# Part of the adaLN modulation of a two-layer backbone: products on GpSimd and VectorE beside the first feed-forward network

## The chip, the cores and the metric

One core of a Trainium2 chip. The metric is the device time of one launch, in microseconds (us). The engines are TensorE (PE in the profile, PEld its weight loads), VectorE (DVE), ScalarE (ACT), GpSimd (POOL) and SyncE (SP). SP issues the large loads, GpSimd issues DMAs of its own.

## The reference, cut to what matters

Two layers over 256 latent and 256 context tokens of width 1024. Every sub-layer is normalised, scaled and shifted by six vectors that come from a conditioning vector, and gated when it is added back:

```python
mod   = silu(c)     @ mod_w + mod_b      # 6 x 1024 for the latent tokens
mod_c = silu(c_ctx) @ mod_w + mod_b      # 6 x 1024 for the context tokens
sh_m, sc_m, g_m, sh_f, sc_f, g_f = split(mod, 6)
h = rmsnorm(x, mix_pre) * (1 + sc_m) + sh_m
x = x + g_m * rmsnorm(mixer(h), mix_post)
h = rmsnorm(x, ffn_pre) * (1 + sc_f) + sh_f
x = x + g_f * rmsnorm(channel_mixer(h), ffn_post)
```

Layer 0 has a pooling and attention mixer and a dense SwiGLU network of hidden width 2816, layer 1 a gated DeltaNet and a top-2-of-8 expert network. The context tokens need no more than the first two vectors of layer 1.

## The kernel before

**Arithmetic.** Every weight slab of [128, 2048] is loaded by SP into a raw buffer and split into a high and a low part, [128, 1024] at a time: ScalarE rounds the high part (L235), VectorE subtracts it (L236, two inputs from SBUF). `wp` has three buffers for each part. A product is three matmuls, L246 to L248 in the up part, L241 to L243 in the down part.

**The first feed-forward network** (`ffn(1, ...)`, the context tokens) takes the 22 blocks of the hidden width two at a time, in eleven steps `s` = 0 to 10. A step is 96 matmuls of 256 columns (up, two slabs), from `s` = 1 on also 24 matmuls of 512 columns (down, one slab, the blocks of step `s`-1), and then `fill(s)`, other work that is put between the steps. A step has six weight halves, so six L235 and six L236. `fill(0)` normalises the latent tokens (its reciprocal root is a `pow` on GpSimd, L261), `fill(1)` transposes them (L293).

**The modulation.** `mod_w` is cut in twelve blocks `j` of 512 columns for each layer; vector `j // 2`, half `j % 2`. `mod_chunk` loads a block as two raw slabs, multiplies it on TensorE with the two conditioning vectors (L415: eight products with 32 columns of weights, each of them two instructions in the trace), copies the sum to SBUF (ScalarE, L433; for the gates, vectors 2 and 5, VectorE adds a bias, L421), and then transposes it into columns (L436, four transposes) or spreads it over the partitions (L430, one product for each conditioning vector) and multiplies by the norm's gain (L431). Before the change a block stands in each `fill(s)` of `s` = 0 to 8; block 10 of layer 0 stands ahead of step 0, and blocks 10, 11, 4 and 5 of layer 1 come in layer 1, from `gates()`.

**The order** of each engine's instructions is made when the program is built: a scheduler with a cost model of its own takes the recorded instructions, and allots the pools' buffers. On the chip every engine keeps that order, and an instruction that waits holds up all that stand behind it on its engine.

Of the kernel before, what the change touches and what calls it, by code (L numbers as in the profile page):

```python
# [10 lines left out]
F32 = mybir.dt.float32  # L11
# [26 lines left out]
NF = 1  # L38
# [71 lines left out]
def _layout(i):  # L110
    """Only data layout: slabs of 128 partitions x 2048 columns, in the order of use."""
# [54 lines left out]
def trunk(ctx, tc, I, out, dbg=None, stop=None):  # L166
# [27 lines left out]
    # ---- constants  # L194
# [31 lines left out]
    # ---- weights: slabs of [128, 2048] from DRAM, then exact high and low parts  # L226
# [12 lines left out]
    def mm3w(ps, ah, al, bh, bl, start, stop):  # L239
        """like mm3, with the low part of b as late as can be"""  # L240
        TE.matmul(ps, ah, bh, start=start, stop=False)  # L241
        TE.matmul(ps, al, bh, start=False, stop=False)  # L242
        TE.matmul(ps, ah, bl, start=False, stop=stop)  # L243
# [6 lines left out]
    # ---- adaLN modulation  # L250
# [3 lines left out]
    # ---- norms  # L254
# [26 lines left out]
    def to_hT(xns, r, ab, ps_of, name):  # L281
        """a stream's normalised tokens, transposed and modulated, as high and low parts; in parts"""
# [21 lines left out]
    def post_begin(ps, grow, ss, w2, junk_of=None):  # L304
        """the sum of squares of a half of y, in PSUM, and that half times its gain"""
        junk = (junk_of or w2)()
        S.activation(junk, ps, AF.Square, accum_out=ss)
        tmp = w2()
        V.tensor_mul(tmp, ps, grow)  # L309
        return tmp  # L310

    def post_end(x_, tmps, ss):
        """x += y * rstd(y)"""
# [7 lines left out]
    def post_residual(x_, halves, grow, w2):  # L321
        """x += (y * rstd(y)) * grow, y in two PSUM tiles."""
# [25 lines left out]
    def hT_tiles(n=T):  # L348
        """high and low parts of a [1024, n] activation, 128 rows to a plane"""
# [10 lines left out]
    def flow(*lanes, lead=False):  # L360
        """traces generators side by side, each at its rate, until all, or the first of them, have ended"""
# [19 lines left out]
    # =================================================== layer 0  # L381
# [27 lines left out]
    def mod_chunk(l, j, load=load, raws=None):  # L409
# [22 lines left out]
        else:  # L432
# [8 lines left out]
            if vec in (1, 4):  # L441
                if half == 0:
# [5 lines left out]
                                       op0=OP.add, op1=OP.mult)  # L448

# [9 lines left out]
    with ExitStack() as mx:  # L459
# [84 lines left out]
        def project():  # L544
            """keys and values, queries, then the channels of the pools"""
# [45 lines left out]
        def softmax(qt, kv):  # L591
            """the probabilities of four heads, rows of queries, in steps"""
# [43 lines left out]
        def read(qt):  # L636
            """the values that eight heads read, rows (group, channel) of the planes of w_out's rows"""
# [62 lines left out]
        early = []  # L700
        for n in range(2):
            for t in order:
                ys[t, n] = psA() if n == 0 else psB()
            for s in range(2):
                raw = slab0(I["w_out"][n, s])
                w = [split_w(raw[:, q * 1024:(q + 1) * 1024]) for q in range(2)]
                if n == 1 and s == 1:
                    early.append(mod_load("l0", 10, slab0))
# [28 lines left out]
    # =============================================== layer 0, FFN  # L737
    by_pow.append(True)

    def ffn(half, acc_of, up_of, load, fill=lambda s: None):  # L740
        """the FFN of one stream, two blocks of the hidden width at a time, in parts"""
# [60 lines left out]
    def fill(s):  # L802
        """other work between the parts of the first stream's FFN"""
# [6 lines left out]
        if mods:  # L810
            mod_chunk(*mods.pop(0), slab0)

    mods = [("l0", 11)] + [("l1", j) for j in (0, 1, 2, 3, 6, 7, 8, 9)]
# [3 lines left out]
    mod_chunk("l0", 10, raws=early.pop())  # L817

    def stream_hT(half, ps_of):
        """the FFN's residual; normalised, modulated and transposed tokens of one stream for layer 1, in parts"""  # L820
# [16 lines left out]
    def both(*gens):  # L837
        """two or more generators in step"""
# [13 lines left out]
    # =================================================== layer 1, gated DeltaNet  # L852
# [46 lines left out]
    def decays(half):  # L899
        """decay and write strength of every token of a stream: columns (direction, tile, head)"""  # L900
# [55 lines left out]
    def blocks(p_, c, half, ps_of):  # L956
        """projection of two heads: [channel, (head, token)]"""
# [10 lines left out]
    def conv_rows(p_, c, half, ps_of):  # L968
        """centred 5-tap convolution along the tokens, 2 * silu, rows of tokens (head, tile)"""
# [21 lines left out]
    def unit_rows(ps, dst, scale):  # L991
        """rows of 128 scaled to the length sqrt(scale); ps holds twice the values"""
# [15 lines left out]
    def staggered(gens, lag):  # L1008
        """traces several generators a step at a time, each lag steps behind the one before"""
# [18 lines left out]
    def project(us, half, ps_of):  # L1028
        """keys of all the pairs of heads first, then the rest; columns (head, tile)"""
# [56 lines left out]
    def scores(u):  # L1086
        """P[j, (direction, head), i] = beta_j (k_j . k_i) decay, strictly before i"""
# [45 lines left out]
    def eliminate(us):  # L1133
        """inverses of the 16 x 16 diagonal blocks of I + P, by elimination on all systems at once"""
# [15 lines left out]
        # forward systems are kept reversed, rows and columns, so that all of them run the same way  # L1150
# [18 lines left out]
    def inverse(u, t):  # L1169
# [26 lines left out]
        # join the two 64 x 64 halves  # L1196
# [28 lines left out]
    def scan(u):  # L1225
        """both directions through the two tiles of a stream, from the state that the last one left"""
# [68 lines left out]
    def gated(u):  # L1295
        """rms norm of every head, gain and gate; transposed parts for the output product"""
# [71 lines left out]
    def gates():  # L1368
        for m in (10, 11, 4, 5):
# [31 lines left out]
    def turned_logits(ps, src, first, last):  # L1401
        """adds the products of 512 channels of a tile of tokens and the router's columns"""
# [10 lines left out]
    def old_logits():  # L1413
        """the router's logits of the tokens before the mixer's part: the gain of the norm goes into the router's
        columns, the shift into a row that is added"""
# [57 lines left out]
    # =================================================== layer 1, experts  # L1473
# [3 lines left out]
    # slabs go round the two pools; a few of the first ones go where nothing else is needed yet  # L1477
# [21 lines left out]
    # the mixer's residual and the norm before the experts; the tokens' logits from those of the two summands  # L1499
# [354 lines left out]
```

## Time and profile before

| | us |
|---|---|
| runs (3) | 2088.44, 2089.57, 2093.78 |
| median | 2089.57 |
| span of the profiled execution | 2088.6 |
| TensorE busy | 1998.0 (96%) |
| VectorE busy | 1590.5 (76%) |
| ScalarE busy | 1354.4 (65%) |
| GpSimd busy | 115.0 (6%) |
| step 0 of the first feed-forward network begins, step 9 ends (TensorE) | 233.3, 440.8 |

How to read it: a matmul's busy time includes its pipeline, so neighbours overlap, and the distance between the starts of two matmuls is what one of them costs TensorE. Idle time matters on the engine that ends a stage. The whole span's averages mix stages of different limits; what counts here is the stretch from 225 to 441 us, in which GpSimd is nearly idle, and the later stretch around 725 to 825 us, in which two of the moved blocks stood.

### The profile page before, as it was taken

What the parts mean: (1) busy time and instruction counts of PE and PEld (TensorE: products, weight loads), DVE (VectorE), ACT (ScalarE), POOL (GpSimd) and SP (SyncE); (2) the same over time, 40 slices, a digit from 0 to 9 for tenths busy, and PEclk for the clock granted to TensorE, in tenths of its full rate; (3) what the DMA queues carried; (4) which work ended last, traced back from release to release, by engine and by line L of the source; (5) the groups of instructions that cost most, each with busy time, mean ns of one, the idle gap of its engine ahead of it and who ended that gap; (6) DMA issues with size and microseconds to landing.
All of it is one profiled execution on the core that took longest, in us unless ns stands there. A gap on an engine that the chain in (4) does not pass through costs nothing. (4 is left out here: it accounts for less than half of the span.)

```text
span 2088.6 us, 30619 instructions
## 1 busy us (share of the span) xinstructions
PE 1998.0 (96%) x11433; PEld 1659.6 (79%) x11433; DVE 1590.5 (76%) x2407; ACT 1354.4 (65%) x2069; POOL 115.0 (6%) x163
## 2 busy tenths in 40 slices
PE   6999899999999899999979999999999999999997
PEld 3746687889999788988868888788887888878785
DVE  3475544456667877886669999899989989899997
ACT  5254543446556566655458878788787777877775
POOL 0000000000001214212000000000000000000000
PEclk9999999999999999999979999999999999999998
DMA  8352467745554344113258999899999999999993
GB/s 352 121 199 80 169 221 260 258 168 170 177 182 162 122 136 168 61 62 104 79 192 309 370 352 361 330 366 374 343 350 350 369 357 354 355 353 369 347 378 124
DMA packets 74076, 519.78 MB, mean 249 GB/s; under 512 B 9456, under 2 KB 9616, under 8 KB 11584
## 3 DMA queue, kind: packets, MB, share of 16 engines
q1 hardware_dynamic: 72864, 515.51, 66.7%
q0 software_dynamic: 1056, 2.24, 0.4%
q8 instruction: 91, 1.49, 0.3%
q14 instruction: 65, 0.53, 0.1%
HBM read 516.67 MB, written 1.05 MB: 248 GB/s over the span
## 5 line engine op out<-in xcount | busy, mean ns | idle before, releaser
L236 DVE TENSOR_TENSOR wlo<-raw,whi 128x1024 fp32r<-128x1024 f32 x878 | 1056.0, 1228 | 266.3 <-ACT whi L235 233.9
L235 ACT ACTIVATE whi<-raw 128x1024 fp32r<-128x1024 f32 x878 | 926.0, 1060 | 467.2 <-PE psA L242 138.7
L243 PE MATMUL psA<-wlo,xh 128*128 128x512 f32 x896 | 354.2, 395 | 2.1 <-DVE wlo L236 2.1
L241 PE MATMUL psA<-whi,xh 128*128 128x512 f32 x896 | 353.3, 395 | 0.3 <-ACT whi L235 0.2
L242 PE MATMUL psA<-whi,xl 128*128 128x512 f32 x896 | 349.9, 391 | 0.0
L241 PE MATMUL psB<-whi,gh 128*128 128x512 f32 x536 | 212.4, 397 | 0.3 <-DVE yacc L1762 0.3
L242 PE MATMUL psB<-whi,gl 128*128 128x512 f32 x536 | 212.1, 396 | 0.0
L243 PE MATMUL psB<-wlo,gh 128*128 128x512 f32 x536 | 210.3, 396 | 0.0
L243 PEld LDWEIGHTS psA<-wlo,xh 128*128 128x128 f32 x896 | 168.2, 188 | 42.3 <-DVE wlo L236 7.5
L241 PEld LDWEIGHTS psA<-whi,xh 128*128 128x128 f32 x896 | 168.2, 188 | 34.8 <-ACT whi L235 1.5
L242 PEld LDWEIGHTS psA<-whi,xl 128*128 128x128 f32 x896 | 168.4, 188 | 33.9 <-DVE xl L1678 0.2
L241 PEld LDWEIGHTS psB<-whi,gh 128*128 128x128 f32 x536 | 100.8, 188 | 23.9 <-issue 0.7
L242 PEld LDWEIGHTS psB<-whi,gl 128*128 128x128 f32 x536 | 100.8, 188 | 23.2
L243 PEld LDWEIGHTS psB<-wlo,gh 128*128 128x128 f32 x536 | 100.3, 188 | 23.8
L246 PE MATMUL psB<-fh,whi 128*128 128x256 f32 x352 | 102.3, 291 | 0.0
L246 PE MATMUL psA<-fh,whi 128*128 128x256 f32 x352 | 100.6, 286 | 0.0
L247 PE MATMUL psB<-fl,whi 128*128 128x256 f32 x352 | 100.3, 285 | 0.0
L248 PE MATMUL psB<-fh,wlo 128*128 128x256 f32 x352 | 100.2, 285 | 0.0
L247 PE MATMUL psA<-fl,whi 128*128 128x256 f32 x352 | 99.6, 283 | 0.0
L248 PE MATMUL psA<-fh,wlo 128*128 128x256 f32 x352 | 99.6, 283 | 0.0
L261 POOL TENSOR_TENSOR rstd<-rstd,mhalf 128x1 f32<-128x1 f32 x17 | 13.1, 774 | 1379.5 <-DVE ss L1509 1005.3
L246 PE MATMUL psB<-jh,whi 128*128 128x256 f32 x256 | 75.6, 295 | 0.0
(474 smaller groups left out, 3447.1 us busy)
## 6 DMA issues: line engine op xcount, KB each, us to landing
raw<-in_moe SPq DMA_DIRECT2D x336, 1024.0 KB, 7.5
raw<-in_ffn SPq DMA_DIRECT2D x66, 1024.0 KB, 4.8
raw<-in_l_mod SPq DMA_DIRECT2D x48, 1024.0 KB, 5.0
raw<-in_w_qkvz SPq DMA_DIRECT2D x24, 1024.0 KB, 4.9
raw<-in_w_out SPq DMA_DIRECT2D x8, 1024.0 KB, 4.8
raw<-in_w_in SPq DMA_DIRECT2D x5, 1024.0 KB, 10.4
w<-in_l_post POOLq DMA_DIRECT2D x8, 256.0 KB, 3.5
x<-in_x SPq DMA_DIRECT2D x2, 512.0 KB, 5.0
```

The lines of the kernel that those rows point to most:

```text
L235: S.activation(hi, src, AF.Copy)
L236: V.tensor_sub(lo, src, f(hi))
L241: TE.matmul(ps, ah, bh, start=start, stop=False)
L242: TE.matmul(ps, al, bh, start=False, stop=False)
L243: TE.matmul(ps, ah, bl, start=False, stop=stop)
L246: TE.matmul(ps, ah, bh, start=start, stop=False)
L247: TE.matmul(ps, ah, bl, start=False, stop=False)
L248: TE.matmul(ps, al, bh, start=False, stop=stop)
L261: G.tensor_tensor(r, r, mhalf[:, 0:n], op=OP.pow)
```

## The change

Twelve blocks, here called c0 to c11, no longer go through `mod_chunk`: c0 and c1 are blocks 10 and 11 of layer 0, c2 to c5 are blocks 0 to 3 of layer 1, c6 to c9 its blocks 6 to 9, c10 and c11 its blocks 10 and 11. The first six have two conditioning vectors, the others one. `mod_begin` loads a block in eight tiles of [128, 512] by DMAs that GpSimd issues, into a pool of six buffers; for the first four tiles GpSimd multiplies by the conditioning vector's column (`tensor_scalar`) and adds to a [128, 512] accumulator (`tensor_tensor`). `mod_end` does the other four tiles on VectorE (`scalar_tensor_tensor`, both tensors in SBUF), then TensorE only sums over the partitions: for the gates by a product with a matrix of ones, otherwise by four transposes for each vector, which VectorE reduces. `fill(s)` begins 1, 1, 1, 1, 1, 2, 2, 2, 0, 0, 0 blocks and ends the oldest ones until two are left open, from `s` = 9 on all. So c0 ends in `fill(1)`, c1 in `fill(2)`, c2 and c3 in `fill(3)` and `fill(4)`, then c4 and c5, c6 and c7, c8 and c9 in pairs, and c10 and c11 in `fill(9)`.

```diff
+NM = 6
+MODS = (1, 1, 1, 1, 1, 2, 2, 2, 0, 0, 0)
+MLAG = 2
...
+    def mod_begin(l, j):
+        vec = j // 2
+        nr = 2 if l == "l0" or vec < 2 else 1
+        if vec in (2, 5):
+            nc.gpsimd.dma_start(bias0[0:1, :], I[l + "_modb"][j:j + 1, :])
+        accs_ = [w2() for r in range(nr)]
+        ws = []
+        for k in range(KD):
+            t = modp.tile([P, 512], F32, tag="modw", name="modw")
+            nc.gpsimd.dma_start(t, I[l + "_mod"][j, k // 4, :, (k % 4) * 512:(k % 4 + 1) * 512])
+            ws.append(t)
+        for k in range(4):
+            for r in range(nr):
+                c_ = cs[:, k, r:r + 1]
+                if k == 0 and vec not in (2, 5):
+                    G.tensor_scalar(accs_[r], ws[k], c_, None, op0=OP.mult)
+                else:
+                    part = modp.tile([P, 512], F32, tag="part", name="part", bufs=1)
+                    G.tensor_scalar(part, ws[k], c_, None, op0=OP.mult)
+                    G.tensor_tensor(accs_[r], accs_[r] if k else bias0, part, op=OP.add)
+        return l, j, accs_, ws[4:]
+
+    def mod_end(begun):
+        l, j, accs_, ws = begun
+        vec, half = j // 2, j % 2
+        for k in range(4, KD):
+            for r, a_ in enumerate(accs_):
+                V.scalar_tensor_tensor(a_, ws[k - 4], cs[:, k, r:r + 1], a_, op0=OP.mult, op1=OP.add)
+        if vec in (2, 5):
...
+                TE.matmul(ps, every, accs_[r], start=True, stop=True)
+                V.tensor_mul(dst, ps, post)
+            return
+        for r, a_ in enumerate(accs_):
+            ps = psB()
+            for b in range(4):
+                TE.transpose(ps[:, b * P:(b + 1) * P], a_[:, b * P:(b + 1) * P], ident)
+            V.tensor_reduce(colm[l][:, vec, half * 4:(half + 1) * 4, r:r + 1],
+                            ps.rearrange("p (b q) -> p b q", b=4), axis=AX.X, op=OP.add)
+        mod_finish_columns(l, vec, half, len(accs_))
...
-                if n == 1 and s == 1:
-                    early.append(mod_load("l0", 10, slab0))
...
-        if mods:
-            mod_chunk(*mods.pop(0), slab0)
-
-    mods = [("l0", 11)] + [("l1", j) for j in (0, 1, 2, 3, 6, 7, 8, 9)]
+        for _ in range(MODS[s]):
+            begun.append(mod_begin(*mods.pop(0)))
+        while len(begun) > (MLAG if s < 9 else 0):
+            mod_end(begun.pop(0))
+
+    mods = [("l0", 10), ("l0", 11)] + [("l1", j) for j in (0, 1, 2, 3, 6, 7, 8, 9, 10, 11)]
+    modp = l0.enter_context(tc.tile_pool(name="modp", bufs=NM))
...
+    begun = [mod_begin(*mods.pop(0))]
...
-    mod_chunk("l0", 10, raws=early.pop())
...
-        for m in (10, 11, 4, 5):
+        for m in (4, 5):
```

The order is the scheduler's, so the diff does not show it. Three places follow, with the program's buffer numbers; the changed kernel has other line numbers. First TensorE at the end of a step `s` = 4, of the kernel before, where a block of layer 1 stands behind the last down matmuls, and its transposes stand right behind its products:

```order
L243 MATMUL psA_2199<-wlo_2816,gh_2606 128x512
L415 MATMUL psB_2835<-raw_2831,cs_101 32x512 x4
L415 MATMUL psB_2835<-raw_2833,cs_101 32x512 x4
L436 MATMUL psB_2846<-cst_74,w2_2844 128x128 x4
L246 MATMUL psB_2857<-fh_1815,whi_2858 128x256
```

and the same place of the changed kernel, where c3's accumulators `w2_2532` and `w2_2533` are transposed:

```order
L243 MATMUL psA_2238<-whi_2957,gh_2713 128x512
L244 MATMUL psA_2238<-whi_2957,gl_2714 128x512
L245 MATMUL psA_2238<-wlo_2958,gh_2713 128x512
L508 MATMUL psB_3019<-cst_74,w2_2532 128x128 x4
L508 MATMUL psB_3025<-cst_74,w2_2533 128x128 x4
L248 MATMUL psB_3035<-fh_1859,whi_3036 128x256
```

The eight products are gone, and TensorE now waits at this place for the accumulators. Second, VectorE of the changed kernel in step 5, around c5 (accumulators `w2_2973` and `w2_2974`; `wlo` are the low parts of the network's weights, `raw_3095` is the second up slab of step 5 and `raw_3161` its down slab):

```order
L238 TENSOR_TENSOR wlo_3099<-raw_3095,whi_3098 128x1024
L456 TENSOR_TENSOR colm_l1_92<-colm_l1_92,modc_l1_90 128x8
L492 SCALAR_TENSOR_TENSOR w2_2973<-modw_2983,cs_101,w2_2973 128x512
L238 TENSOR_TENSOR wlo_3127<-raw_3095,whi_3126 128x1024
L492 SCALAR_TENSOR_TENSOR w2_2974<-modw_2983,cs_101,w2_2974 128x512
L492 SCALAR_TENSOR_TENSOR w2_2973<-modw_2985,cs_101,w2_2973 128x512
L492 SCALAR_TENSOR_TENSOR w2_2974<-modw_2985,cs_101,w2_2974 128x512
L238 TENSOR_TENSOR wlo_3164<-raw_3161,whi_3163 128x1024
```

A block's sums now stand between the low parts, so a low part that TensorE needs in this step stands behind a sum that needs GpSimd's part. Third, GpSimd of the changed kernel, from the last two instructions of c2 (`w2_2314`) into c3 (tiles `modw_2534` on), with what each waits for:

```order
L484 TENSOR_TENSOR w2_2314<-w2_2314,part_2348 128x512 [waits Pool_49]
L474 DMA modw_2536<-in_l1_mod 128x512
L474 DMA modw_2538<-in_l1_mod 128x512 [waits DMASW5_49,DVE_49]
L480 TENSOR_SCALAR w2_2532<-modw_2534,cs_101 128x512 [waits DMASW2_49,Activation_49]
L480 TENSOR_SCALAR w2_2533<-modw_2534,cs_101 128x512 [waits Activation_49]
L474 DMA modw_2540<-in_l1_mod 128x512 [waits DMASW6_49,DVE_49]
L474 DMA modw_2542<-in_l1_mod 128x512 [waits Pool_49]
L483 TENSOR_SCALAR part_2552<-modw_2536,cs_101 128x512 [waits DMASW3_49]
L496 DMA w2_2578<-in_l0_post 128x512 [waits DMASW7_49,Activation_49]
L484 TENSOR_TENSOR w2_2532<-w2_2532,part_2552 128x512 [waits Pool_49]
```

Before, GpSimd had nothing in this stretch but two small DMAs and a few `pow`. Now its loads of c3 stand between its products, and the third and fourth of them wait for VectorE to be done with the buffers of c2.

## Rows read from the trace of the kernel before

**Rows 1.** The page's busy times over the span, of TensorE and GpSimd.

```profile
PE 1998.0 (96%) x11433; PEld 1659.6 (79%) x11433; DVE 1590.5 (76%) x2407; ACT 1354.4 (65%) x2069; POOL 115.0 (6%) x163
```

**Rows 2.** Busy time by stretch: length, PE, PEld, DVE, ACT, POOL, clock, DMA share.

```profile
325.00:350.00 25.00, 24.28 (x181) 21.41 (x180) 11.10 (x14) 10.41 (x13) 0.00 (x0) 1.00 0.74 264
```

**Rows 3.** Timeline of TensorE in the first feed-forward network: start, length, instruction.

```profile
227.42 3.64 PE L415 MATMUL psB<-raw,cs 128*32 128x512 f32 x16 [0.20 <-ACT w L296]
231.00 0.86 PE L293 MATMUL psB<-cst,w 128*128 128x128 f32 x4
...
301.20 0.66 PE L436 MATMUL psB<-cst,w 128*128 128x128 f32 x4 [0.72 <-ACT w L433]
...
313.20 0.40 PE L241 MATMUL psA<-whi,gh 128*128 128x512 f32 x1
...
318.90 1.92 PE L415 MATMUL psB<-raw,cs 128*32 128x512 f32 x16
321.54 0.66 PE L436 MATMUL psB<-cst,w 128*128 128x128 f32 x4 [0.72 <-ACT w L433]
...
339.23 1.92 PE L415 MATMUL psB<-raw,cs 128*32 128x512 f32 x16
...
440.81 0.28 PE L246 MATMUL psB<-fh,whi 128*128 128x256 f32 x1
```

**Rows 4.** What TensorE waited for from 218 to 450 us: total, times, longest.

```profile
PE psB L436 <- ACT w L433: 7.2, 8, 2.2
PE psB L430 <- DVE rstd L260: 4.0, 1, 4.0
```

**Rows 5.** Instructions of GpSimd over the span: nanoseconds min/median/max; a landing; a pow.

```profile
L1178 POOL TENSOR_TENSOR w<-w,cst x8: 1273/1292/1507, 799.5 to 909.3; 128x512 f32<-128x512 f32 x8
...
L1175 POOL TENSOR_TENSOR u<-w,cst x32: 716/736/1729, 697.4 to 993.0; 128x256 f32<-128x256 f32 x32
...
L1106 POOL TENSOR_SCALAR_AFFINE_SELECT x<-x x12: 401/408/412, 599.8 to 882.9; 128x256 f32<-128x256 f32 x12
...
L424 POOL DMA_DIRECT2D w<-in_l_post x8: 547/600/673, 108.5 to 811.5; - x8
...
DMA to landing us min/median/max: 3.3/3.5/7.1
...
251.95 0.58 POOL L261 TENSOR_TENSOR rstd<-rstd,mhalf 128x1 f32<-128x1 f32 x1
```

**Rows 6.** VectorE: the low parts from 225 to 430 us, and a two-input sum of 512.

```profile
L236 DVE TENSOR_TENSOR wlo<-raw,whi x53: 1224/1226/1227, 237.7 to 427.8; 128x1024 fp32r<-128x1024 f32 x53
...
L985 DVE SCALAR_TENSOR_TENSOR u<-u,u x20: 680/685/1215, 543.0 to 956.6; 128x512 f32<-128x512 f32 x20
```

**Rows 7.** Timelines of GpSimd and VectorE where both work, in layer 1.

```profile
961.91 1.30 POOL L1178 TENSOR_TENSOR w<-g,cst 128x512 f32<-128x512 f32 x1
963.16 3.53 POOL L1178 TENSOR_TENSOR w<-x,cst 128x512 f32<-128x512 f32 x2
...
963.45 2.10 DVE L236 TENSOR_TENSOR wlo<-raw,whi 128x1024 fp32r<-128x1024 f32 x1 [4.11 <-ACT whi L235]
...
987.01 7.13 POOL L1175 TENSOR_TENSOR u<-w,cst 128x256 f32<-128x256 f32 x8
...
990.66 1.76 DVE L236 TENSOR_TENSOR wlo<-raw,whi 128x1024 fp32r<-128x1024 f32 x1 [1.14 <-PE psB L248]
992.35 1.21 DVE L1319 TENSOR_TENSOR yl<-u,yh 128x512 fp32r<-128x512 f32 x1
```

**Rows 8.** Layer 1 from 725 to 825 us: sum over four stretches of 25; one group.

```profile
sum 100.00, PE 95.09 PEld 82.27 DVE 74.84 ACT 62.70 POOL 22.92; mean PE 23.77 PEld 20.57 DVE 18.71 ACT 15.67 POOL 5.73
...
L430 PE MATMUL psB<-w,cst 128*128 128x512 f32 x8 | 4.1, 593 | 0.0
```

More of the change, by code (lines that the diff above doesn't have):

```diff
@@ L37 @@
 NX = 2
-NF = 1
+NM = 6
+MODS = (1, 1, 1, 1, 1, 2, 2, 2, 0, 0, 0)
+MLAG = 2
 Q0, Q1, Q2 = 1.0, 0.5, 0.25
@@ L448, in mod_chunk, with mod_finish_columns @@
                                        op0=OP.add, op1=OP.mult)
+    def mod_finish_columns(l, vec, half, nr):
+        ks = slice(half * 4, (half + 1) * 4)
+        cv = colm[l][:, vec, ks, 0:nr]
+        V.tensor_add(cv, cv, modc[l][:, vec, ks, None].to_broadcast([P, 4, nr]))
+        if vec in (1, 4):
+            if half == 0:
+                A = cp.tile([P, KD, 2], F32, name=f"A_{l}{vec}")
+                AB[l, vec // 3] = (A, colm[l][:, vec - 1])
+            pre_b = pre[l][:, vec // 3, ks, None].to_broadcast([P, 4, nr])
+            V.scalar_tensor_tensor(AB[l, vec // 3][0][:, ks, 0:nr], cv, 1.0, pre_b, op0=OP.add, op1=OP.mult)
@@ new lines, in mod_end @@
+    def mod_end(begun):
[5 more added lines that the diff above has]
+        if vec in (2, 5):
+            post = w2()
+            src = I[l + "_post"][vec // 3:vec // 3 + 1, half * 512:(half + 1) * 512]
+            nc.gpsimd.dma_start(post, src.to_broadcast([P, 512]))
+            for r in range(2 if l == "l0" else 1):
+                key = (l, vec, r)
+                dst = glast[:, half * 512:(half + 1) * 512] if key == ("l1", 5, 0) else w2()
+                rows.setdefault(key, []).append(dst)
+                ps = psB()
[3 more added lines that the diff above has]
+        for r, a_ in enumerate(accs_):
+            ps = psB()
+            for b in range(4):
[3 more added lines that the diff above has]
+        mod_finish_columns(l, vec, half, len(accs_))
@@ L698, in begin @@
             tmps[t, n] = post_begin(ys[t, n], rows["l0", 2, 0 if t < 2 else 1][n], sss[t][:, n:n + 1], w2)
-        early = []
         for n in range(2):
@@ L809, in fill @@
                 pass
-        if mods:
-            mod_chunk(*mods.pop(0), slab0)
-    mods = [("l0", 11)] + [("l1", j) for j in (0, 1, 2, 3, 6, 7, 8, 9)]
+        for _ in range(MODS[s]):
[4 more added lines that the diff above has]
+    modp = l0.enter_context(tc.tile_pool(name="modp", bufs=NM))
+    bias0 = modp.tile([P, 512], F32, name="bias0", bufs=1)
+    G.memset(bias0, 0.0)
+    every = C("iota")[:, 1:2].to_broadcast([P, P])
+    begun = [mod_begin(*mods.pop(0))]
     for _ in to_hT([xnf[2], xnf[3]], 1, AB["l0", 1], psB, "f"):
```

## The prediction

> **What bounds the kernel now.** I read the busy times first: TensorE is busy for 96% of the span, GpSimd for 6% [rows 1]. An average says little about one stage, so next the stretch of the first feed-forward network: from 325 to 350 us TensorE is busy for 24.28 of 25 us at full clock, VectorE for 11.10, ScalarE for 10.41, GpSimd for nothing [rows 2]. TensorE bounds this stage, and its timeline shows what a modulation block costs there [rows 3]: its products start at 318.90, its transposes at 321.54 and end at 322.20. That is 3.3 us, of which the products take 1.92 and a wait for ScalarE's copy 0.72. The next block starts at 339.23, so a step without one takes 17.0 us; its up part takes 11.3 (301.86 to 313.20). The waits list says that TensorE waits for little else here: 7.2 us for the copies, once 4.0 for a bias [rows 4]. Step 9 ends at 440.8 [rows 3]; behind it the two kernels do the same, but for two blocks in layer 1. So the question is when step 9 ends after the change.
>
> **TensorE's own part.** With the products gone, step 0 starts behind the last four transposes of the context tokens, at 227.4 + 0.9 = 228.3 [rows 3]. Then come 11.3 for step 0, 9 x 17.0 for steps 1 to 9, 2.6 for the 16 transposes of the latent tokens and 7.9 for the 48 transposes that the change keeps (0.66 for four [rows 3]; the four blocks c2 to c5 have eight now, the next four have four), and 6.2 for six sums of the gates' blocks (eight instructions, two to a product, took 4.1 [rows 8]). The sum is 409.6: **31 us earlier** than 440.8, if nothing that TensorE waits for is late. What follows asks that.
>
> **GpSimd's part.** A sum of two tensors of 512 columns takes 1.29, of 256 columns 0.74 [rows 5], so 0.18 is fixed and 0.55 goes by 256 columns. A multiplication by a column is not in the trace. It has one tensor in; the nearest row is the select, 0.41 for 256 columns. With the same fixed part, 512 columns take 0.63, which I take: the select also has one tensor in. The bounds are 0.41 (the select as it stands) and 1.29 (two inputs). Issuing a DMA holds GpSimd for 0.60, and it lands 3.5 after that starts [rows 5]. A two-vector block is 8 x 0.63 + 6 x 1.29 + 8 x 0.60 = 17.6 us of GpSimd, more than a step of TensorE; a one-vector block 4 x 0.63 + 3 x 1.29 + 8 x 0.60 = 11.2; c10 and c11 have one sum and a small DMA more, 13.0.
>
> These blocks form a chain. There are six buffers for eight tiles, and the last four are held until VectorE has done its sums, which wait for GpSimd's; so GpSimd's loads of the next block wait for VectorE's sums of this one, in GpSimd's queue, ahead of its products. c0 is done early: its loads wait for nothing of the network. c1 is held by two `pow` that stand in GpSimd's queue ahead of its second sum. The second ended at 252.5 before [rows 5], 7 us behind step 0; now step 0 ends at 239.6, so 246. Behind it c1 has 7 sums, 6 multiplications and 3 loads left, 14.6: done at 260.6. I walked down GpSimd's order for each block behind it, and let a load start when its buffer is free. c2 to c5 take 4 x 17.6 and 11.5 more, c6 to c11 take 4 x 11.2 + 2 x 13.0 and 9.5 more; most of the surplus is 2 to 3.5 us in which the second tile, loaded too late, has not landed. That puts the end of GpSimd's part of c11 at 422.8, without any collision.
>
> **Collisions.** When a low part started at 963.45, inside a sum of GpSimd, it took 2.10 instead of 1.23 [rows 6, 7]; the sum behind it had to wait in turn, and GpSimd's two took 3.53 instead of 2.58 [rows 5, 7]. Each waits for the other. From 987.01 eight sums of 256 columns took 7.13 instead of 5.89, beside 1.92 us of VectorE's two-input work [rows 5 to 7]. So each microsecond of such work beside GpSimd costs GpSimd 0.65 (here) to 0.77 (there). A two-vector block has 8 sums of 0.69, 6 low parts of 1.23 and one of 0.69 on VectorE, 13.5 us. About three quarters meet GpSimd's products, at 0.65 6.6 us; some of that falls into the waits for landings, and I take 5.3. A one-vector block has half of it beside fewer products, 2.6. With 4.0 for c1 that is 4.0 + 4 x 5.3 + 6 x 2.6 = 40.8, so c11's part ends at **463.6**.
>
> The Trainium skill states a stricter rule (SBUF — State Buffer, Who interferes with whom): a VectorE instruction with two SBUF inputs and a GpSimd instruction that reads SBUF exclude each other for the whole instruction. By that rule, from 246 on, 105 us of GpSimd's products and 106 of VectorE's two-input work (46 low parts, 60 sums, 12 others) stand one behind the other, c11 would be done at 457, and the time would be 2120. The rows bear the exclusion out.
>
> **The end of step 9.** c11's sums stand on VectorE behind the first low part of step 9 and ahead of its second one. So TensorE gets that low part two sums and 1.23 later, 2.6; then three quarters of step 9's up part and the down part, 14.2, and the two gate sums, 2.1. That is 463.6 + 18.9 = 482.5, **42 us later** than 440.8. TensorE idles in steps 2 to 9, waiting for low parts that stand behind VectorE's sums; its 31 us are gone in that.
>
> **The rest.** In layer 1 two blocks go: 2 x 1.92 and two sums of 1.03 on TensorE, 5.8 us. TensorE is busy there for 95.09 of 100 us, VectorE for 74.84 [rows 8], so between 0 (VectorE ends a part of it) and 5.8; I take 4. SP's loads are 24 slabs fewer, which nothing waited for. The bytes are the same. The sum is 42 - 4 = 38 us more. The profiled span, 2088.6, is 1.0 below the median of the runs, 2089.6, to which I add it: **2127**.
>
> The Trainium skill calls GpSimd's one-input operations roughly line-rate (GPSIMD Engine Reference, Engine selection): at the 1.2 GHz of its Specifications an estimate of 0.43 for 512 columns. No row shows it; with it the 62 multiplications from c1's rest on would cost 12 less, and the sum would be 2115.
>
> **The rivals.** *The chain stays hidden.* To keep all of the 31 us, c11's part would have to be done by 409.6 - 18.9 = 390.7, 32 before my sum without collisions. Multiplications of 0.41 give 14 of that, loads that land in time (the surplus of 21) the rest: then 2053, with 5.8 in layer 1. For it: VectorE has 14 of 25 us free [rows 2]. Against: the collisions of rows 7 would have to vanish too. The point is 390.7. With multiplications of 0.41 alone and no collision it is 2073. Chance of 2053 to 2080: 0.17.
>
> *The chain just keeps pace.* Without collisions step 9 ends at 441.7, 1 later than before, and layer 1 gives 4: 2087. For it: GpSimd's wait may fall together with the landings. Chance of 2080 to 2097: 0.15.
>
> *GpSimd is slower yet.* Collisions at 0.77 over all of VectorE's two-input work (38 more), multiplications of twice the select, 0.81 (11 more), landings of 5 instead of 3.5, as the 7.1 in rows 5 allows, in eight blocks (12 more): 2188. Waits between dependent products, of which the trace has none, go the same way. Chance of 2160 and more: 0.20.
>
> **How the numbers follow.** The forecast, a chain of GpSimd and VectorE that TensorE waits for, has 2097 to 2160 and a chance of 0.48. A measurement of this kernel can tell about 0.3%, 6 us, from no change. Faster than 2083: the first rival and a little of the second, 0.19. Within 6 us: 0.11. Slower: 0.70. The range from 2070 to 2190 leaves out about 0.1 on each side; the forecast's own is 2097 to 2160.
>
> **What would show it.** If I am right, step 9 ends near 482 on TensorE; GpSimd is busy nearly all the time from 246 to 464; low parts on VectorE take 1.5 to 2.3 where they took 1.23; TensorE's waits in steps 2 to 9 are put down to low parts (or ScalarE's high parts behind them), and the longest waits of VectorE are for GpSimd's accumulators, and of GpSimd for landings of `modw`. A multiplication takes 0.6. I am wrong if VectorE's sums start without a wait, if TensorE's steps keep their 17 to 18 us, or if the low parts stay at 1.23.

## The result, and the profile after

| | before | after |
|---|---|---|
| median, us (4 runs each) | 2091.02 | 2191.05 |
| lowest to highest, us | 2088.44 to 2093.78 | 2188.01 to 2193.24 |
| span of the profiled execution, us | 2088.6 | 2186.3 |
| step 0 begins, step 9 ends (TensorE), us | 233.3, 440.8 | 223.8, 529.5 |
| from there to the end of the span, us | 1647.8 | 1656.8 |

The change makes the kernel **4.8% slower**: ratio 1.0482, 95% interval 1.0470 to 1.0494. The direction and the mechanism are those of the prediction, the size is not: 100 us instead of 38. Step 9 ends 47 us later than predicted, and the part behind it is 13 us longer than predicted.

The page's busy times, the answer to [rows 1]:

```profile
PE 1998.4 (91%) x11257; PEld 1673.2 (77%) x11257; DVE 1671.1 (76%) x2479; ACT 1353.3 (62%) x2063; POOL 382.5 (17%) x392
```

TensorE has no less busy time than before: it has fewer matmuls, but runs many of them at a lower clock. The stretch of [rows 2], of the changed kernel (stretch, length, busy PE, PEld, DVE, ACT, POOL, clock, DMA share, GB/s):

```profile
325.00:350.00 25.00, 16.46 (x81) 14.67 (x82) 14.74 (x18) 5.15 (x6) 22.05 (x17) 0.73 0.43 148
```

TensorE now runs 81 matmuls where it ran 181 (both in 25 us), at a granted clock of 0.73, and GpSimd is the engine that is busy nearly all the time (22.05 of 25 us). What the engines waited for from 218 to 560 us (engine, line, releaser: total, times, longest):

```profile
ACT whi L237 <- PE psB L249: 140.3, 38, 14.0
DVE w L492 <- POOL w L484: 104.0, 18, 13.3
...
PE psB L250 <- DVE wlo L238: 59.9, 12, 10.6
...
PE psA L245 <- DVE wlo L238: 26.1, 8, 7.9
```

The chain reads from right to left: VectorE's sums (L492) wait 104 us for GpSimd's accumulators, TensorE waits 86 us for low parts (L238), which stand behind those sums on VectorE and have next to nothing else to wait for. ScalarE's 140 us only pass it on. One link of it on the timelines of GpSimd, VectorE and TensorE (start, length, instruction):

```profile
395.50 1.57 POOL L483 TENSOR_SCALAR part<-modw,cs 128x512 f32<-128x512 f32 x1
397.15 1.26 POOL L484 TENSOR_TENSOR w<-w,part 128x512 f32<-128x512 f32 x1
398.51 3.17 POOL L483 TENSOR_SCALAR part<-modw,cs 128x512 f32<-128x512 f32 x1
```
```profile
398.44 0.75 DVE L492 SCALAR_TENSOR_TENSOR w<-modw,cs,w 128x512 f32<-128x512 f32 x1 [9.52 <-POOL w L484]
399.11 1.22 DVE L238 TENSOR_TENSOR wlo<-raw,whi 128x1024 fp32r<-128x1024 f32 x1
```
```profile
400.39 0.58 PE L250 MATMUL psB<-fh,wlo 128*128 128x256 f32 x1 [9.54 <-DVE wlo L238]
```

GpSimd's sum ends at 398.41; VectorE, idle for 9.52 us, does one sum and then the low part that TensorE has been idle for, 9.54 us. The instructions of GpSimd, the answer to [rows 5] (count, ns min/median/max, first and last start):

```profile
L483 POOL TENSOR_SCALAR part<-modw,cs x60: 1558/1570/3541, 174.1 to 507.0; 128x512 f32<-128x512 f32 x60
```
```profile
L480 POOL TENSOR_SCALAR w<-modw,cs x12: 1575/1784/2262, 283.6 to 460.4; 128x512 f32<-128x512 f32 x12
```

Here is the miss: a **multiplication takes 1.57 us** where the prediction took 0.63, and never less than 1.558. It costs more than a sum of two tensors (1.29). The end of the chain, on GpSimd, VectorE and TensorE:

```profile
508.69 1.26 POOL L484 TENSOR_TENSOR w<-w,part 128x512 f32<-128x512 f32 x1
```
```profile
509.98 1.54 DVE L492 SCALAR_TENSOR_TENSOR w<-modw,cs,w 128x512 f32<-128x512 f32 x2 [7.76 <-POOL w L484]
511.43 1.22 DVE L238 TENSOR_TENSOR wlo<-raw,whi 128x1024 fp32r<-128x1024 f32 x1
```
```profile
512.71 0.58 PE L250 MATMUL psB<-fh,wlo 128*128 128x256 f32 x1 [6.69 <-DVE wlo L238]
...
528.20 1.88 PE L502 MATMUL psB<-w,cst 128*128 128x512 f32 x4
529.51 0.68 PE L248 MATMUL psB<-fh,whi 128*128 128x256 f32 x1
```

c11's part is done at 509.9 (predicted 463.6), and step 9 ends 19.6 us later (predicted 18.9).

### The profile page after: what moved, and what is told of

It reads as the page before. It is cut to its first block, busy times and chain, and to the rows that moved or that the text cites. A ratio compares the mean times of both kernels' runs of the same rounds, so it can differ in the third digit from the quotient of the medians.

```text
span 2186.3 us, 30640 instructions
## 1 busy us (share of the span) xinstructions
PE 1998.4 (91%) x11257; PEld 1673.2 (77%) x11257; DVE 1671.1 (76%) x2479; ACT 1353.3 (62%) x2063; POOL 382.5 (17%) x392
## 3 DMA queue, kind: packets, MB, share of 16 engines
HBM read 516.66 MB, written 1.05 MB: 237 GB/s over the span
## 5 line engine op out<-in xcount | busy, mean ns | idle before, releaser
L238 DVE TENSOR_TENSOR wlo<-raw,whi 128x1024 fp32r<-128x1024 f32 x878 | 1062.0, 1235 | 177.3 <-ACT whi L237 141.6
L250 PE MATMUL psB<-fh,wlo 128*128 128x256 f32 x352 | 108.3, 308 | 59.9 <-DVE wlo L238 59.9
L492 DVE SCALAR_TENSOR_TENSOR w<-modw,cs,w 128x512 f32<-128x512 f32 x72 | 62.9, 893 | 104.4 <-POOL w L484 104.0
L250 PEld LDWEIGHTS psB<-fh,wlo 128*128 128x128 f32 x352 | 74.9, 213 | 62.3 <-DVE wlo L238 62.3
L483 POOL TENSOR_SCALAR part<-modw,cs 128x512 f32<-128x512 f32 x60 | 111.7, 1862 | 11.1 <-DMA modw<-in_l_mod 7.2
L248 PE MATMUL psB<-fh,whi 128*128 128x256 f32 x352 | 108.0, 308 | 2.3 <-ACT fh L300 1.2
L249 PE MATMUL psB<-fl,whi 128*128 128x256 f32 x352 | 106.1, 302 | 1.3 <-DVE fl L301 1.3
```

The lines of the kernel that those rows point to most:

```text
L238: V.tensor_sub(lo, src, f(hi))
L249: TE.matmul(ps, ah, bl, start=False, stop=False)
L250: TE.matmul(ps, al, bh, start=False, stop=stop)
L483: G.tensor_scalar(part, ws[k], c_, None, op0=OP.mult)
L492: V.scalar_tensor_tensor(a_, ws[k - 4], cs[:, k, r:r + 1], a_, op0=OP.mult, op1=OP.add)
```

## The experiments

In all of them the scheduler makes the order of the engines anew; where it stays as it was, the text says so. Every ratio is to the kernel before on the same chip, which had a median of 2089.3 to 2089.7 us. Where no number of runs is given, the version ran twice, and its ratio is good to between 0.2 and half a per cent. "c11's part" is GpSimd's part of the last block; it ends at 509.9 us in the changed kernel, and step 9 there at 529.5.

**Is it the price of the product? The same product in another form.** The first product of a block, which goes straight into the accumulator, is changed in the same way.

```diff
-G.tensor_scalar(part, ws[k], c_, None, op0=OP.mult)
+G.tensor_tensor(part, ws[k], c_.to_broadcast([P, 512]), op=OP.mult)
```

> GpSimd's multiplications are written as a product of two tensors, the column spread over 512 columns (the same values; the order of all engines stays). If the change is slow because GpSimd's own work sets the pace and the form with a column costs 1.57 us (theory), a product costs what a sum costs, 1.29: 62 x 0.28 = 17 us less, 2174 us, and step 9 ends near 512. If the pace is set by waits between the engines and not by GpSimd's work (rival), the time stays at 2186 to 2196 whatever a product costs. If an operand that is one column is what is slow, in either form, a product stays at 1.57 or more, and so does the time.

2170.99 us, ratio 1.0381 (1.0331 to 1.0431): 20 us less than the changed kernel, with the order of VectorE, ScalarE and GpSimd unchanged. GpSimd's products and sums in this run, from their lines:

```profile
L483 POOL TENSOR_TENSOR part<-modw,cs x60: 1029/1052/2658, 178.9 to 491.7; 128x512 f32<-128x512 f32 x60
```
```profile
L484 POOL TENSOR_TENSOR w<-w,part x54: 1260/1302/2281, 187.1 to 492.8; 128x512 f32<-128x512 f32 x54
```

A product of two tensors, one of them a spread column, costs 1.05, less than the 1.29 that was expected, and less than the same product as a `tensor_scalar`. 62 x 0.52 = 32 us were to be had; step 9 ended 15.5 us earlier. GpSimd waited for buffers 30.5 us instead of 10.8, and VectorE's low parts became slower. The two kernels' low parts from 239 to 530 us, first of this run, then of the changed kernel (line, shape, count | busy, mean ns | idle before):

```profile
L238 DVE TENSOR_TENSOR wlo<-raw,whi 128x1024 fp32r<-128x1024 f32 x63 | 102.5, 1629 | 14.2 <-ACT whi L237 14.2
```
```profile
L238 DVE TENSOR_TENSOR wlo<-raw,whi 128x1024 fp32r<-128x1024 f32 x57 | 73.6, 1294 | 6.6 <-ACT whi L237 6.6
L492 DVE SCALAR_TENSOR_TENSOR w<-modw,cs,w 128x512 f32<-128x512 f32 x70 | 61.0, 893 | 99.6 <-POOL w L484 99.3
```

**Is the column the costly operand?**

```diff
-G.tensor_scalar(part, ws[k], c_, None, op0=OP.mult)
+G.tensor_scalar(part, ws[k], 0.5, None, op0=OP.mult)
```

> GpSimd multiplies by the number 0.5 instead of the conditioning vector's column (left out: half of the modulation's products are not by the vector). If the column as an operand is what makes a multiplication cost 1.57 us, it costs 0.63 to 0.81 here, 62 x 0.8 to 0.9 less, and the time is 2135 to 2145. If the form costs 1.57 whatever it multiplies by, nothing moves: 2186 to 2196.

2182.33 us, ratio 1.0435 (1.0386 to 1.0485), 4 us below the second of the two ranges. A multiplication by a number has a median of 1.505 us, 0.065 less than by a column. It is the form that costs, not the column.

**With the price that the prediction took.** `part` stays one tile, cleared once.

```diff
-G.tensor_scalar(part, ws[k], c_, None, op0=OP.mult)
+G.tensor_scalar(part[:, 0:176], ws[k][:, 0:176], c_, None, op0=OP.mult)
```

> 60 of GpSimd's 72 multiplications take 176 of their 512 columns (left out: the products of the others), so that one costs about the 0.63 us that the prediction took. Theory (the product's price is the error of the prediction): of the 62 behind the start of the chain 50 are cheaper by 0.94, 47 us less: step 9 ends near 482 and the time is 2135 to 2150. Rival (the pace is set by buffers, landings and VectorE's order, so GpSimd would only wait longer): less than 20 us of it come back, 2170 or more.

2160.81 us, ratio 1.0333 (1.0277 to 1.0388), and step 9 ends at 501.8.

```profile
L483 POOL TENSOR_SCALAR part<-modw,cs x60: 719/731/2778, 177.4 to 475.6; 128x176 f32<-128x176 f32 x60
```

A multiplication takes 0.73, not the 0.63 that was aimed at: 50 x 0.84 = 42 us cheaper, of which 27.7 reached the end of step 9. By the letter neither range was met. c11's part ends at 477.6, 32 us earlier. The rest of the 42 us goes mainly into more waits of GpSimd (for landings 10.7 us instead of 6.5) and into the twelve multiplications that were left whole (mean 2.15 instead of 1.88). Step 9 then ends 24.2 us behind c11's part instead of 19.6, since c11's sums now stand in step 8 and a whole step follows.

**Do the six buffers tie GpSimd to VectorE?**

```diff
-NX = 2
+NX = 1
-NM = 6
+NM = 10
```

> The pool of tiles has ten buffers instead of six, and the pool of raw slabs one instead of two to make room. From 246 to 510 us GpSimd waits 12 us for VectorE to free a buffer and 7 for landings. Theory (GpSimd's own work, 236 of 264 us, sets the pace): at most these 19 us come back, 2172 to 2186. Rival (the six buffers tie GpSimd to VectorE and are the cause): 2140 or less.

2188.44 us, ratio 1.0465 (1.0414 to 1.0515): step 9 ends at 530.3. The waits for landings are gone. GpSimd still waits for buffers that VectorE frees (13.4 us from 246 to 512 us, 10.8 in the changed kernel), c11's part ends 5 us earlier, and step 9 does not. So four buffers more bring nothing, which speaks against the rival; the run does not show what GpSimd would do without any wait for a buffer.

**What is there to gain without the chain?** No product on GpSimd, one on VectorE for each vector.

```diff
 def mod_begin(l, j):
-    for k in range(4):
...
-    return l, j, accs_, ws[4:]
+    return l, j, accs_, ws
...
 def mod_end(begun):
...
-    for k in range(4, KD):
-        for r, a_ in enumerate(accs_):
-            V.scalar_tensor_tensor(a_, ws[k - 4], cs[:, k, r:r + 1], a_, op0=OP.mult, op1=OP.add)
+    for r, a_ in enumerate(accs_):
+        V.tensor_scalar(a_, ws[r], cs[:, r, r:r + 1], None, op0=OP.mult)
```

> GpSimd only loads the tiles, and VectorE multiplies one tile for each vector and sums nothing (left out: seven of the eight products of each moved block, so the modulation is another one). TensorE has the work of the changed kernel and nearly nothing to wait for. If the 31 us that the prediction gave TensorE are there, step 9 ends near 410. Behind it the changed kernel took 1657 us, the kernel before 1648: if the 9 more come from layer 1 without the blocks c10 and c11 there, the time is 2067 to 2072; if they were a late effect of the chain, 2058 to 2062.

2080.62 us (8 runs), ratio 0.9956 (0.9944 to 0.9968): 9 us more than the upper of the two ranges. Step 9 ended at 422.7, not 410. Step 0 took 15.0 instead of 11.3, its first 5 us at a clock of 0.50; TensorE waited 6.5 us for a tile that landed late; step 8 ran at 0.87. So of the 31 us that the prediction gave TensorE, 18 are there, and behind step 9 another 7 are lost. The last number also answers the other question: 7 of the changed kernel's 9 us behind step 9 are there without the chain, so they are no late effect of it. Even with the chain all but gone the change brings 0.4%.

**Two blocks back to layer 1.**

```diff
-MODS = (1, 1, 1, 1, 1, 2, 2, 2, 0, 0, 0)
+MODS = (1, 1, 1, 1, 1, 2, 2, 0, 0, 0, 0)
...
-        for m in (4, 5):
+        for m in (10, 11, 4, 5):
```

> The blocks c10 and c11 go back to TensorE and to layer 1, where they were before; c0 to c9 stay with GpSimd and VectorE. In the changed kernel GpSimd's part of c9 ended at 473.8; two more steps of TensorE behind it give 515 to 522 for the end of step 9, against 529.5. Theory (layer 1 without the two blocks is what got longer): the part behind step 9 is back at 1646 to 1650, 2165 to 2174 in all. Rival (it is longer for another reason): 1655 to 1658 behind it, 2175 to 2181.

2171.44 us, ratio 1.0391 (1.0350 to 1.0431). Step 9 ends at 516.8, and from there the span has 1651.4 more: between the two theories. Split at VectorE's last products with the gates it is clear: up to there 1640.1, as before (1640.0), and in the changed kernel 1644.2; behind them 11.3, before 7.8, in the changed kernel 12.6. So the 9 us have two parts, 4.2 and 4.8, and in this run the first is gone. That it goes with the two blocks is not shown: the two versions at the end of this section leave layer 1 as it was and have 3 us of it too (below).

**A better share of the tiles.** `range(2)` and `ws[2:]` in `mod_begin`, sums from tile 2 on in `mod_end`, and GpSimd's product as a product of two tensors.

> GpSimd takes two of a block's eight tiles, VectorE six, and GpSimd multiplies as a product of two tensors (1.05 us in the run column_as_tensor, 1.57 as a tensor_scalar). GpSimd then has 36 x 1.05 + 24 x 1.29 + 96 x 0.57 = 124 us in the twelve blocks, less than TensorE's ten steps; VectorE 108 sums of 0.75, 57 low parts of 1.23 and some 30 us more, 181, about as much as TensorE (409 - 239 = 170). Theory (the chain was too long because of GpSimd's products): step 9 ends at 425 to 440, 2080 to 2097 us. Rival (the order of VectorE, sums ahead of low parts, makes TensorE wait as long as sums wait for GpSimd at all): 2120 or more.

2120.77 us, ratio 1.0148 (1.0110 to 1.0186), step 9 ends at 464: 70 us better than after, and by the letter the rival's time. The rival's reason is a part of it only: TensorE waits 21 us for low parts instead of 86. GpSimd is busy for 121 of 223 us, about as worked out; VectorE for 201 instead of the 181 that were worked out, since beside products of two tensors its own two-input instructions are slower (low parts 1.42, sums 0.93). VectorE is now the engine that is busy most, and GpSimd waits 42 us for buffers that it frees.

**All on VectorE.**

```diff
-        for k in range(4):
...
-        return l, j, accs_, ws[4:]
+        return l, j, accs_, ws
...
-    for k in range(4, KD):
+    for k in range(KD):
         for r, a_ in enumerate(accs_):
-            V.scalar_tensor_tensor(a_, ws[k - 4], cs[:, k, r:r + 1], a_, op0=OP.mult, op1=OP.add)
+            c_ = cs[:, k, r:r + 1]
+            if k == 0 and vec not in (2, 5):
+                V.tensor_scalar(a_, ws[k], c_, None, op0=OP.mult)
+            else:
+                V.scalar_tensor_tensor(a_, ws[k], c_, a_ if k else bias0, op0=OP.mult, op1=OP.add)
```

> GpSimd only loads; VectorE does all eight tiles of each block. VectorE has 144 sums of 0.75, 57 low parts of 1.23 and some 30 us more, 208 us from 239 on: more than TensorE's 170. Theory (whoever has more than TensorE's 17 us a step sets the pace): step 9 ends at 440 to 455, 2095 to 2112 us, and no low part takes more than 1.23. If the sums on VectorE hide (TensorE bound): step 9 ends at 410 and 2067.

(A gate's block reads its bias in `mod_end` here, when that of a later block may already stand in `bias0`; the work is the same.) 2175.76 us, ratio 1.0411 (1.0375 to 1.0448), step 9 ends at 517.7. The price of an instruction was right, the rest not: low parts take 1.22 and sums 0.74, but VectorE is busy for only 190 of 275 us. With six buffers for eight tiles, the last loads of a block wait for the block's first sums (GpSimd waits 127 us for them), and TensorE's transposes stand behind the last sum. What TensorE waited for:

```profile
PE psB L503 <- DVE w L487: 56.8, 8, 10.4
PE psB L497 <- DVE w L487: 27.1, 4, 10.5
```

**The loads issued by SP.**

```diff
-nc.gpsimd.dma_start(t, I[l + "_mod"][j, k // 4, :, (k % 4) * 512:(k % 4 + 1) * 512])
+nc.sync.dma_start(t, I[l + "_mod"][j, k // 4, :, (k % 4) * 512:(k % 4 + 1) * 512])
```

> The changed kernel, its 96 loads of tiles issued by SP instead of GpSimd. The loads held GpSimd for 47.6 us from 246 to 512 and let it wait 14.9 more. Theory (GpSimd's own work sets the pace, its issues a part of it): 45 to 60 us come back, step 9 ends at 470 to 485, 2125 to 2145 us. Rival (a load that waits for a buffer holds up the network's weights behind it in SP's queue): TensorE waits for weights instead, 2165 or more. In all runs with 96 loads by GpSimd the span ends 12.6 us behind VectorE's last products with the gates, before it was 7.8: if the use of GpSimd's queue is the reason, it is 7.8 here; if not, 12.6.

2161.68 us, ratio 1.0347 (1.0328 to 1.0366). c11's part ends at 482.8, 27 us earlier; step 9 only 20 us earlier, at 509.4, since c11's sums now stand in step 8 and a whole step of 20 us follows. At step 9 that is less than half of what was expected, and TensorE does not wait for weights; its longest waits are still for low parts (57 us). With no loads in its queue, GpSimd's products meet VectorE's work more (mean 2.09 instead of 1.87) and wait for more landings (13.5 us). The question on the end of the span has a clear answer. VectorE's last products with the gates, of the changed kernel and of this run (x4: durations, first and last start), and this run's span:

```profile
L311 DVE TENSOR_TENSOR m<-yacc,glast x4: 684/685/694, 2171.9 to 2173.7; 128x512 f32<-128x512 f32 x4
```
```profile
L311 DVE TENSOR_TENSOR m<-yacc,glast x4: 684/684/691, 2151.4 to 2153.2; 128x512 f32<-128x512 f32 x4
```
```profile
core 0: 2161.0 us, clock 0.964
```

From the last one's start to the end of the span: 12.6 us in the changed kernel (2186.3), 7.8 here.

**GpSimd without VectorE's sums.** `range(4, 5)` instead of `range(4, KD)` in `mod_end`.

> VectorE sums one of its four tiles for each vector (left out: three of a block's eight products), and the buffers of the other three are free as they land; GpSimd has all its work. Its instructions at their medians (1.57, 1.29, 0.57) make 24.9 for a two-vector block, 14.7 for a one-vector block, 17 for c10 and c11, 192 us behind c1, which ended at 278: c11 would end at 470 with no waits and no collisions, and it ended at 510. Theory (GpSimd's work is the pace, the 40 us are collisions and waits in about equal parts, and VectorE's sums cause half of the first and most of the second): c11 ends at 482 to 495, 2158 to 2172 us. If VectorE's sums are what mainly holds TensorE up: step 9 ends below 460, less than 2120. If they cost nothing: 2186 to 2196.

2221.34 us, ratio 1.0633 (1.0613 to 1.0652), outside all three expectations. The experiment put in a wait of its own: a buffer that nobody reads is free when its load has landed, so the next load waits for that on GpSimd's queue (54 us in all), ahead of GpSimd's products. What it does show is how the two engines meet, at 426 us, on GpSimd and VectorE:

```profile
426.31 2.69 POOL L483 TENSOR_SCALAR part<-modw,cs 128x512 f32<-128x512 f32 x1
```
```profile
426.44 1.22 DVE L238 TENSOR_TENSOR wlo<-raw,whi 128x1024 fp32r<-128x1024 f32 x1
```

GpSimd's multiplication started first and lost 1.12 us; the low part started second and lost nothing.

**Two versions that are faster than both kernels.** They start from the kernel before and move only c6 to c9, the blocks with one vector; the two-vector blocks and layer 1 stay as they were. The order of the blocks is mixed: block 11 of layer 0; 6 and 0 of layer 1; then 1, 7, 2, 8, 3, 9, one to a step. The first:

```diff
...
+    def mod_vector(l, j):
+        raws = mod_load(l, j, slab0)
+        acc = w2()
+        for k in range(KD):
+            w_ = raws[k // 4][:, (k % 4) * 512:(k % 4 + 1) * 512]
+            if k == 0:
+                V.tensor_scalar(acc, w_, cs[:, k, 0:1], None, op0=OP.mult)
+            else:
+                V.scalar_tensor_tensor(acc, w_, cs[:, k, 0:1], acc, op0=OP.mult, op1=OP.add)
+        return l, j, acc
...
```

> The kernel before, in which only the four blocks with one vector of the first feed-forward network (c6 to c9) leave TensorE: VectorE multiplies and sums all eight tiles from the raw slabs that SP loads (8 x 0.7 = 5.6 us a block), GpSimd has nothing, and the order of blocks is mixed so that such a block stands in every second step. TensorE saves 3.3 - 0.66 = 2.6 us a block, 10.6; VectorE has 14 of 25 us free and no one to wait for. Theory (what is moved is worth it where the receiver has room and needs no third engine): 2079 us, 0.5% less than before. Rival (sums ahead of low parts make TensorE wait even so): 2087 to 2095.

**2078.85 us** (6 runs), ratio **0.9943** (0.9926 to 0.9960), as expected. Step 9 ends at 429.1, 11.7 us earlier. Its low parts and sums from 240 to 432 us, and a stretch as in [rows 2]:

```profile
L236 DVE TENSOR_TENSOR wlo<-raw,whi 128x1024 fp32r<-128x1024 f32 x57 | 69.7, 1224 | 59.2 <-ACT whi L235 59.2
L476 DVE SCALAR_TENSOR_TENSOR w<-raw,cs,w 128x512 f32<-128x512 f32 x28 | 20.9, 748 | 0.3
```
```profile
350.00:375.00 25.00, 25.00 (x166) 22.13 (x169) 18.21 (x24) 11.51 (x14) 0.00 (x0) 1.00 0.71 258
```

TensorE is busy all the time at full clock, the sums wait for next to nothing (0.3 us), and before the low parts VectorE is idle for 59 us until their high parts are there. The second gives the same blocks to GpSimd, as in the changed kernel's `mod_begin` but for all eight tiles, one vector, and the product of two tensors:

> The same four blocks, all eight tiles on GpSimd, as products of two tensors (1.05 each) and sums of 1.29, with tiles that GpSimd loads: 8 x 1.05 + 7 x 1.29 + 8 x 0.57 = 22 us a block, 88 in about 150. Its slack is two steps a block, VectorE has no sums. Theory (a chain that ends within its slack costs nothing): 2079 to 2083, the low parts on VectorE slower and hidden. Rival (the collisions with VectorE's low parts reach TensorE): 2088 or more.

2080.89 us (5 runs), ratio 0.9959 (0.9944 to 0.9973), step 9 ends at 428.4.

```profile
325.00:350.00 25.00, 24.28 (x181) 21.41 (x180) 18.30 (x15) 9.38 (x13) 23.59 (x19) 1.00 0.81 299
```

GpSimd is as busy as in the changed kernel (23.59 of 25), VectorE's low parts are slowed by it (mean 1.53 instead of 1.22), and TensorE does not wait for one of them: here GpSimd has two steps for a block of 26 us, and no low part stands behind an instruction that waits for it. The two versions' intervals overlap; which is the faster is open.

## Why the prediction failed in size

**What bounds it: right.** The signs of the chain are there: GpSimd busy for 236 of 264 us from 246 to 510; VectorE's longest waits for accumulators; TensorE's for low parts; step 9 ends 19.6 us behind c11's part. The rival of a chain that stays hidden falls with c11's part at 509.9 instead of 390.7.

Three of the signs that were named are not there. A multiplication does not take 0.6. GpSimd waits longer for buffers (12.0 us) than for landings (6.5). And the low parts do not take 1.5 to 2.3: of 57, only 6 take 1.5 or more, and the median stays where it was, which by the prediction's own words speaks against its collisions (from 239 to 530 us: ns min/median/max):

```profile
L238 DVE TENSOR_TENSOR wlo<-raw,whi x57: 1160/1218/2299, 242.0 to 529.3; 128x1024 fp32r<-128x1024 f32 x57
```

**The step that failed: "A multiplication by a column is not in the trace ... 512 columns take 0.63".** It measured 1.57, outside even the bound of 1.29 "(two inputs)". The select, from which the price came, has one tensor in as well, but the number of inputs does not set the price: the same product costs 1.05 with two tensors and 1.5 to 1.57 with one. 62 of them stand behind the start of the chain: 62 x 0.94 = 58 us, more than the 46.3 by which c11's part is late; other terms, below, take some of it back. That this price is the main cause is shown by the two runs that make the product cheaper: 32 us cheaper gave 20 of time, 42 gave 30, and the second brings c11's part to 477.6, with twelve dear products left. They also show the limit of the sum: in a chain of three engines a saved microsecond is worth some 0.6 to 0.7, so step 9 still ends at 501.8 there and not at the 482.5 that was predicted.

The Trainium skill's rule (GPSIMD Engine Reference, Engine selection) that a one-input operation of GpSimd is roughly line-rate, by which the sum would have been 2115, is contradicted by the row: 1.57, not 0.43. By the same section a two-input one is about twice as slow as on VectorE; 1.29 against 0.69 [rows 5, 6] agrees; the product of two tensors, 1.05, is nearer to 1.5 times.

**The rival that named the number: luck.** "GpSimd is slower yet" gave 2188 with a chance of 0.20, and 2191 was measured. Of its three terms only the dearer multiplication is there, at five times its size (58 us instead of 11); its stronger collisions and later landings are not. That its sum fits is luck.

**c0 and c1: off.** "c0 is done early" was wrong with the dearer product: in step 0 its sums waited 4.7 us on VectorE ahead of a low part, TensorE's step 0 ended at 241.2 instead of 239.6, and the second `pow` at 253.9 instead of 246. That made c1 7.7 us later beyond its own products.

**Collisions: half.** Predicted 40.8 for GpSimd. From 246 to 512 us the 51 multiplications of L483 have a mean of 1.868, 0.30 above the median, the 12 of L480 0.31, the sums 0.04: 51 x 0.30 + 12 x 0.31 + 52 x 0.04 = 21 us. The waits for buffers and landings were right (20 us measured, 21 predicted). So the sum to c11's part is: products +58, c1 +8, collisions -20, loads 83 x (0.574 - 0.600) = -2: 44 of the 46.3 us between 463.6 and 509.9.

**"The rest ... I take 4" (less): wrong by 13 us.** From the end of step 9 to the last products with the gates the changed kernel takes 4.2 us more than the kernel before, not 4 less. All ten kernels that move the two blocks take 1.2 to 4.2 us more, and the one that puts them back 0.1. But the two versions at the end of the last section, which leave layer 1 as it was, take 3.2 and 3.0 us more too. The products of the kernel before and of the first of these versions, whose step 9 ends at 440.8 and 429.1:

```profile
L309 DVE TENSOR_TENSOR m<-yacc,glast x4: 681/684/692, 2079.0 to 2080.8; 128x512 f32<-128x512 f32 x4
```
```profile
L309 DVE TENSOR_TENSOR m<-yacc,glast x4: 684/686/692, 2070.6 to 2072.4; 128x512 f32<-128x512 f32 x4
```

So a difference of this size comes without moving the two blocks, and its cause stays open. Lower clocks are seen where it arises. In the changed kernel TensorE waits 2 us once for ScalarE, and then runs at a granted clock of 0.69; stretches of the changed kernel:

```profile
922.00:927.00 5.00, 3.04 (x25) 2.75 (x24) 1.70 (x8) 4.86 (x15) 0.44 (x1) 1.00 0.00 0
927.00:932.00 5.00, 5.00 (x32) 5.00 (x33) 3.97 (x17) 2.45 (x5) 0.00 (x0) 0.69 0.01 3
```

The same place of the kernel before had 1.00 throughout. What is shown is that the gain of 4 us is not there. The other 4.8 us lie at the very end and come from GpSimd's loads, below; the prediction has no term for them, since it took the kernels to be the same behind step 9 but for the two blocks.

## What to carry to other kernels

Price an operation on an engine by the form of the instruction that will run, not by its number of inputs. Where the trace has no row of that form, rows of other forms do not bound it (1.57 lay above the dearest of them, 1.29); a run of that one instruction settles it. Work that is taken from the bounding engine pays if the receiver ends within its own slack and nothing that the bounding engine needs is queued behind a wait for it; a third engine in between (here VectorE's sums between GpSimd's) turns slack into a chain. Move as much as fits: four blocks gave 0.4 to 0.6% where twelve cost 4.8%.

## What the runs showed of the hardware

- **GpSimd's `tensor_scalar` is slow**: 128 x 512 by a column 1.57 us, by a number 1.505, as a product with a spread column 1.05; a sum of two tensors 1.29.
- **Who yields depends on GpSimd's form.** Beside `tensor_scalar` VectorE's low parts hardly slow down (mean 1.29) and GpSimd's instruction is stretched while VectorE works, also where GpSimd started first. Beside products of two tensors the low parts have a mean of 1.53 to 1.63, and they lose also where VectorE started first: in the run with the product in another form one low part took 4.65 us, while two products and a sum that GpSimd started inside it kept their 1.0 and 1.28 (VectorE, then GpSimd):

```profile
344.27 4.65 DVE L238 TENSOR_TENSOR wlo<-raw,whi 128x1024 fp32r<-128x1024 f32 x1
```
```profile
344.55 2.04 POOL L480 TENSOR_TENSOR w<-modw,cs 128x512 f32<-128x512 f32 x2
346.55 1.28 POOL L484 TENSOR_TENSOR w<-w,part 128x512 f32<-128x512 f32 x1
```

  The Trainium skill's rule (SBUF — State Buffer, Who interferes with whom) is that the one that starts first holds the port for the whole instruction. Neither this low part of 4.65 us nor GpSimd's multiplication of 2.69 us at 426.31, in the run without most of VectorE's sums, fits it: each started first and lost.
- **The end of the span grows with GpSimd's loads.** From the last product with the gates to the end: 7.8 us before and with SP's loads, 7.9 with 32 loads by GpSimd, 11.3 with 80, 12.6 with 96 in all nine kernels that have them. What the device does there, the trace does not show.
